# mLSTM rows stored chunk by chunk, the first head's masks spread, the first modulation in halves, and a head's queries and keys as transfers to all 128 partitions

## The chip, the core and the metric

The kernel runs as one program on one core of a Trainium2 chip. The core has five engines with instruction streams of their own: TensorE (PE in the profile; PEld is its loading of weights), VectorE (DVE), ScalarE (ACT), GpSimd (POOL) and SyncE (SP). It also has 16 DMA engines, which move data between HBM and the on-chip memory SBUF. In this kernel SP does almost nothing but issue DMAs, one behind the other, in the order of the program; GpSimd issues a few more. The metric is the device time of one execution in microseconds (us). SBUF has 128 partitions, and a tile is written here as partitions x elements.

## The reference, cut to what matters

One layer works on 2048 latent rows of 1024 features (a grid 64 wide), with 256 rows of context in front. Its steps are these:

1. A conditioning vector `c` (for the context `c_ctx`) goes through SiLU and a matrix `w_ada` to give shift, scale and gate (the modulation).
2. The normalised rows, shifted and scaled, go through one input projection `w_in`. Its columns feed two groups of heads.
3. Group A is neighbourhood attention: 8 heads of 64 features. Every latent row reads a clamped window of 8 x 16 rows with a learned bias, and all context rows, in one softmax.
4. Group B is an mLSTM: 4 heads of 128 features, in both directions, in chunks of 128 rows, with a state carried from chunk to chunk.
5. Both outputs go through an output projection, a normalisation, and a mixture of experts with another normalisation.

```
q, k, v = heads(z)                       # group A, 8 heads of 64
p = softmax([q . k_window + bias, q . k_ctx]);  o = p . [v_window, v_ctx]
for chunk in 16 chunks of 128 rows:      # group B, 4 heads of 128, two directions
    h = (decay * (q k^T)) v + q C        # C: the state so far
    C = f * C + k^T v
```

## The kernel before, in words

The stages follow each other on the core. The first modulation and the first rows take the first 41 us. The input projection runs to 793 us. The mLSTM runs from 793 to 973 us in 32 steps (16 chunks, two directions in turn). The neighbourhood attention runs from 973 to 1280 us in 8 heads of 16 blocks. The output projection and the router follow until about 1600 us, and the mixture of experts takes the rest.

The projection keeps float32 accuracy by splitting each value in a high and a low part. It leaves the attention's queries in DRAM as `qhi` and `qlo` and the keys as `khi` and `klo` (128 rows each: two heads of 64 features). The mLSTM's queries and keys lie in `mqk_d` (L57) as [128 features, 2, 4 heads, 2304 rows].

*The mLSTM loop* is at L857 to L875. Turn n fetches the operands of step n+3 (`fetch_step`, L100 to L108: `qk` from `mqk_d`, the broadcast gate rows `bcs`, the values `va`), then takes one piece of the generator `head(0)`, which loads the first attention head, and then computes. The tiles `qk` and `bcs` have three buffers each. VectorE forms the decayed weights (L796: `ex` from `bcs`, four instructions a step), multiplies them with the scores (L816) and updates the state (L784). GpSimd scales values and queries (L802, L808).

*A head's load* is the generator `head(h)` (L703 to L748). It puts, in this order, on SP's stream: `qhi` and `qlo` (64 rows of 8192 bytes each, to partitions 0-63 and 64-127 of the tile `qkk`), `khi` twice and `klo` twice (64 rows of 9216 bytes each, to both halves), nine `bias` tiles, `vc`, and sixteen pieces of the values `vw`. After the fourth bias load GpSimd adds the window's mask to a bias tile (L721), one in each further piece. The attention loop (L1047 to L1083) takes two pieces of the next head's generator in each of its turns, so a head's loads are put on SP's stream while the head before it is computed. The tiles of a head exist twice (`kps[h % 2]`).

*The order on SP* is the program's. All these loads go through one queue, and a later issue stands behind an earlier one that waits.

*Transfers with a written-out source.* Some loads name their source as a list of [step, count] pairs, outermost first. A bias load (L732) has 16 x 8 rows of 384 or 512 elements. The gates are read back for the mLSTM's scans (L273, L274) as 4 heads x 16 chunks x 128 elements, to 64 partitions:

```
src = bass.AP(tensor=gd.tensor, offset=off, ap=[[NT, 4], [P if d == 0 else -P, n], [1, P]])
```

*The first modulation* (L185 to L220) loads `c` and `c_ctx` with one feature to a partition, then all 32 pieces of `w_ada` (128x512, 256 KB each); four products run beside each other on PE for each of eight k. Only then come four transposes, and after them the first rows are transposed and projected (L246 to L248). The weights `w_in` of the projection come by `load_w` (L227).

Of the kernel before, what the change touches and what calls it, by code (L numbers as in the profile page):

```python
# [11 lines left out]
F32 = mybir.dt.float32  # L12
# [4 lines left out]
AF = mybir.ActivationFunctionType  # L17
OP = mybir.AluOpType
# [4 lines left out]
P = 128  # L23
D = 1024
KC = D // P
SEQ = 2048
# [9 lines left out]
def tile_layer(ctx, tc, A, out):  # L36
    nc = tc.nc

    def in_order(i):
        return tc.keep_in_program_order(i)  # L40
# [11 lines left out]
    qhi_d = [dram.tile([P, SEQ], F32, name=f"qhi{i}") for i in range(4)]  # L52
    qlo_d = [dram.tile([P, SEQ], F32, name=f"qlo{i}") for i in range(4)]
# [3 lines left out]
    mqk_d = dram.tile([P, 2, 4, NT], F32, name="mqk_d")  # L57
# [54 lines left out]
    with ExitStack() as es, ExitStack() as zes:  # L112
# [72 lines left out]
        def first_modulation():  # L185

            cc = stp.tile([P, 2, KC], F32, name="cc", bufs=1)
            nc.sync.dma_start(cc[:, 0, :], A["c"].rearrange("o (k p) -> p (o k)", p=P))
            nc.sync.dma_start(cc[:, 1, :], A["c_ctx"].rearrange("(k p) -> p k", p=P))
            nc.gpsimd.memset(cs[:], 0.0)  # L190
            for i in range(2):
                nc.scalar.activation(cs[:, :, i], cc[:, i, :], AF.Silu)
            pa = pt.tile([P, 2, 2, P], F32, name="ptx")
            pa = pa[:].rearrange("p a b t -> p (a b t)")
            for i in range(2):
                bada = zp.tile([1, 1024], F32, name=("cosq", "sinq")[i])
                nc.sync.dma_start(bada[:], A["b_ada"][:, i * 1024 : (i + 1) * 1024])
                for j in range(2):
                    c0 = 64 * i + 32 * j
                    nc.tensor.matmul(  # L200
                        pa[c0 : c0 + 32, :], ones1[:], bada[:, j * 512 : (j + 1) * 512], start=True, stop=False, tile_position=(0, c0)
                    )
            for k in range(KC):
                wts = []
                for j in range(4):
                    wt = xg.tile([P, 512], F32, name=f"x{('hi', 'lo')[j // 2]}_{j % 2}_{k}")
                    nc.sync.dma_start(wt[:], A["w_ada"][0, k * P : (k + 1) * P, j * 512 : (j + 1) * 512])
                    wts.append(wt)
                for j in range(4):
                    nc.tensor.matmul(  # L210
                        pa[32 * j : 32 * j + 32, :], cs[:, k, :], wts[j][:], start=False, stop=k == KC - 1, tile_position=(0, 32 * j)
                    )
            rows = tp.tile([P, 512], F32, name="t")
            nc.vector.tensor_copy(rows[:], pa)
            pm = pt.tile([P, 2, 2, P], F32, name="ptx")
            pm = pm[:].rearrange("p a b t -> p (a b) t")
            for q in range(4):
                nc.tensor.transpose(pm[:, q, :], rows[:, q * P : (q + 1) * P], ident[:])
            nc.vector.tensor_copy(modT[:, :, 0:64], pm[:, :, 0:64])
            nc.vector.tensor_scalar(modT[:, :, 64:P], pm[:, :, 64:], 1.0, None, OP.add)  # L220

        def weights(c0):

            his, los = [], []
            return his, los, c0
# [146 lines left out]
        def context_state():  # L372
# [3 lines left out]
            for i in range(2):  # L376
                c = 16 + i
                nc.sync.dma_start(kt[:, i], mqk_d[:, 1, :, c * P : (c + 1) * P])
                nc.gpsimd.memset(va[i][:, :, 128:129], 1.0)
                nc.sync.dma_start(va[i][:, :, 0:P], mv_d[c * P : (c + 1) * P, :].rearrange("p (h d) -> p h d", h=4))  # L380
# [98 lines left out]
        def rows_of_x(half, q):  # L479
            r0 = half * 1024 + q * 512  # L480
            return load_rows(A["x"][0, r0 : r0 + 512], 4, (["x"] * 3 + spare)[4 * q :])

        xq = [normalised(rows_of_x(0, 0))]
        first_modulation()
# [10 lines left out]
        for half in range(2):  # L495
# [18 lines left out]
            w = weights(0)  # L514
            if half:
                load_w(w)
            for q, (g, n, t0) in enumerate(groups[0:2]):
                pss = []
                for k2 in range(0, KC + 2, 2):
                    if half == 0 and q == 0 and k2 < KC:  # L520
                        load_w(w, (k2, k2 + 1))
                    built(g, k2 // 2 + 1)
                    if half or k2 == KC:
                        built(groups[1][0], k2 // 2 + 1 if half else 1)
                    if k2 == 2:
                        pss = [pz.tile([P, 512], F32, name="ps") for _ in range(4)]
                    if k2:
                        for c in range(4):
                            mm_T(pss[c][:], g, w, c * P, (k2 - 2, k2 - 1))
                    if half == 0 and q == 0 and k2 == 2:  # L530
                        rows_of[1] = normalised(rows_of_x(0, 1), True)
# [58 lines left out]
            for qk in range(2):  # L590
# [5 lines left out]
                for h in range(4):  # L596
# [3 lines left out]
                    for g, n, t0 in groups:  # L600
# [38 lines left out]
                        if t0 == SEQ:  # L639
                            nc.vector.tensor_scalar(acc[:, 0:m], acc[:, 0:m], P ** -0.5, None, OP.mult)  # L640
                            nc.sync.dma_start(mqk_d[:, 1, h, SEQ:NT], acc[:, 0:m])
                            continue
# [7 lines left out]
                        nc.sync.dma_start(mqk_d[:, qk, h, o0:o1], t1[:, 0:m])  # L650
# [47 lines left out]
    heads = {}  # L698

    def load(dst, src):  # L700
        in_order(nc.sync.dma_start(dst, src))

    def head(h):  # L703
# [5 lines left out]
        load(q[0:64, :].bitcast(F32), qhi_d[pair][f0 : f0 + 64, :])  # L709
        yield  # L710
        load(q[64:P, :].bitcast(F32), qlo_d[pair][f0 : f0 + 64, :])
        yield
        for dst, src in ((ka, khi_d), (kb, klo_d)):
            for p0 in (0, 64):
                load(dst[p0 : p0 + 64, :].bitcast(F32), src[pair][f0 : f0 + 64, :])
            yield
        bias = []

        def masked(i):
            w = (12, 16, 12)[i // 3] * 32  # L720
            in_order(nc.gpsimd.tensor_tensor(bias[i][:, 0:w], bias[i][:, 0:w], mask[:, i, 0:w], OP.add))  # L721
# [186 lines left out]
    with ExitStack() as es:  # L908
# [139 lines left out]
        for n in range(128 + 6):  # L1048
# [1171 lines left out]
```

## Time and profile before

| | |
|---|---|
| time, median of 3 runs | 2725.88 us (2724.01 to 2726.02) |
| the profiled execution's own time | 2719.89 us |
| its span, first to last instruction | 2717.9 us |
| mean granted clock of TensorE | 0.962 |
| PE, DVE, ACT, POOL busy | 91%, 47%, 30%, 28% of the span |
| DMA traffic, mean | 231 GB/s |

PE is busy for most of the span as a whole, but the stages differ. The share of the span says nothing of a single stage; each is read by itself, from its own stretch, with the wait that ends last there. The chain of waits that ended last, in the page, holds only the last DMAs of the mixture of experts, so it tells nothing of the stages in which the change lies.

### The profile page before, as it was taken

Reading aid. Unit: us, or ns where it says so; the run is one execution under the profiler, and the core shown is the slowest. Engines: PE = TensorE matmul, PEld = TensorE weight load, DVE = VectorE, ACT = ScalarE, POOL = GpSimd, SP = SyncE. Lnnn points to the kernel's source line nnn. Section 1 sums busy time; section 2 is a strip of 40 time slices with the busy share of each in tenths; the row PEclk is TensorE's granted clock in tenths of the full one; section 3 lists DMA queues with packets and bytes.
Section 4 is the critical chain, followed back from the end, with each engine's and each line's share of the span. In section 5 each row is a group of like instructions: output and inputs, shape, how many; then the busy total and the mean of one; then the engine's idle time right before and its main releaser. Section 6 shows DMA issues by size and latency. Waiting matters only on the chain. (4 is left out here: it accounts for less than half of the span.)

```text
span 2717.9 us, 51820 instructions
## 1 busy us (share of the span) xinstructions
PE 2481.7 (91%) x17292; PEld 1568.7 (58%) x17292; DVE 1268.3 (47%) x2882; ACT 804.9 (30%) x1707; POOL 759.1 (28%) x886
## 2 busy tenths in 40 slices
PE   8999999999997899998999679979999999999890
PEld 4778667877887778876787533323333333333330
DVE  5547224257236976665578952222222233222226
ACT  4423105243134666655565310000000000000005
POOL 1212211002034535456434422211222122221124
PEclk9999999999999999999999779989999999999995
DMA  8634762334449979994654689999689886998936
GB/s 268 178 102 134 248 219 94 140 97 158 112 137 260 265 197 214 202 212 141 183 152 151 213 308 349 366 394 340 220 281 335 312 299 223 331 328 318 381 102 263
DMA packets 286891, 626.97 MB, mean 231 GB/s; under 512 B 79448, under 2 KB 142924, under 8 KB 262444
## 3 DMA queue, kind: packets, MB, share of 16 engines
q1 hardware_dynamic: 254716, 564.87, 62.6%
q0 software_dynamic: 31696, 60.09, 9.6%
q8 instruction: 70, 1.15, 0.2%
q10 hardware_dynamic: 352, 0.39, 0.1%
q14 instruction: 57, 0.47, 0.1%
HBM read 947.01 MB, written 97.42 MB: 384 GB/s over the span
## 5 line engine op out<-in xcount | busy, mean ns | idle before, releaser
L2048 POOL DMA_INDIRECT acc_d<-y,ids x112 | 174.6, 1559 | 739.9 <-DMA acc_d<-y,ids 277.7
L2011 DVE TENSOR_TENSOR sg<-sg,ph 128x128 f32<-128x128 f32 x112 | 39.8, 355 | 442.7 <-ACT sg L2010 427.2
L2010 ACT ACTIVATE sg<-ph 128x128 f32<-128x128 f32 x112 | 37.1, 331 | 690.5 <-PE ph L2005 522.3
L2005 PE MATMUL ph<-qkk,xT 128*64 128x512 f32 (+1 forms) x1344 | 233.9, 525 | 2.8 <-DMA qkk<-in_w_dram 2.8
L2005 PE MATMUL ph<-mask,xT 128*64 128x512 f32 x896 | 210.8, 613 | 21.5 <-DMA mask<-in_w_dram 21.5
L246 PE MATMUL ps<-xhi,whi 128*128 128x512 f32 (+1 forms) x576 | 221.7, 386 | 1.7 <-DVE ev L509 1.6
L247 PE MATMUL ps<-xlo,whi 128*128 128x512 f32 (+1 forms) x576 | 220.4, 383 | 0.2 <-DVE xlo L182 0.2
L248 PE MATMUL ps<-xhi,wlo 128*128 128x512 f32 (+1 forms) x576 | 220.2, 382 | 0.0
L2037 PE MATMUL py<-mo,gT 128*64 128x512 f32 x672 | 166.2, 631 | 24.4 <-DMA mask<-in_w_dram 12.3
L255 PE MATMUL ps<-whi,xhi 128*128 128x512 f32 x416 | 166.1, 401 | 1.5 <-ACT whi L234 1.5
L256 PE MATMUL ps<-wlo,xhi 128*128 128x512 f32 x416 | 164.3, 396 | 3.2 <-DVE wlo L235 3.2
L257 PE MATMUL ps<-whi,xlo 128*128 128x512 f32 x416 | 164.8, 397 | 0.0
L960 DVE CUSTOM_DVE_ANT_0 sb<-ps,bias 128x640 f32<-128x640 f32 (+1 forms) x128 | 113.9, 891 | 102.9 <-PE ps L957 82.7
L2005 PEld LDWEIGHTS ph<-mask,xT 128*64 128x64 f32 x896 | 61.8, 140 | 144.5 <-issue 142.8
L2005 PEld LDWEIGHTS ph<-qkk,xT 128*64 128x64 f32 (+1 forms) x1344 | 74.9, 128 | 114.4 <-issue 98.5
L2021 DVE COPY gT<-pg 128x128 f32<-128x128 f32 x112 | 40.2, 359 | 210.6 <-PE pg L2019 205.7
L1972 DVE TENSOR_SCALAR xT<-pxt,mod 128x96 f32<-128x96 f32 x456 | 135.0, 369 | 2.5 <-PE pxt L1965 2.5
L246 PEld LDWEIGHTS ps<-xhi,whi 128*128 128x128 f32 x576 | 108.3, 188 | 28.7 <-issue 3.2
L2045 DVE SCALAR_TENSOR_TENSOR y<-py,wgt,g2r 128x256 f32<-128x256 f32 x112 | 68.7, 613 | 119.9 <-PE py L2037 119.9
L2010 ACT ACT_TABLE_LOAD x28 | 35.9, 1283 | 299.5 <-PE ph L2005 299.5
L247 PEld LDWEIGHTS ps<-xlo,whi 128*128 128x128 f32 x576 | 108.3, 188 | 23.0 <-DVE xlo L182 0.9
L248 PEld LDWEIGHTS ps<-xhi,wlo 128*128 128x128 f32 x576 | 108.3, 188 | 23.0 <-DVE wlo L235 0.3
(549 smaller groups left out, 5087.2 us busy)
## 6 DMA issues: line engine op xcount, KB each, us to landing
w<-in_w_dram SPq DMA_DIRECT2D x203, 1024.0 KB, 7.5
mask<-in_w_dram SPq DMA_DIRECT2D x114, 1024.0 KB, 8.7
qkk<-in_w_dram SPq DMA_DIRECT2D x114, 1024.0 KB
mo<-in_w_dram SPq DMA_DIRECT2D x171, 512.0 KB, 4.1
bias<-in_w_dram SPq DMA_DIRECT2D x58, 1024.0 KB
xo<-in_w_dram SPq DMA_DIRECT2D x115, 512.0 KB, 8.2
bias<-in_w_dram SPq DMA_DIRECT2D x58, 512.0 KB
qkk<-in_w_dram SPq DMA_DIRECT2D x58, 512.0 KB
```

What stands on the lines that cost most here:

```text
L246: nc.tensor.matmul(ps, wh_, xhi[g, k][:], start=k == 0, stop=False)
L247: nc.tensor.matmul(ps, wh_, xlo[g, k][:], start=False, stop=False)
L248: nc.tensor.matmul(ps, wl_, xhi[g, k][:], start=False, stop=k == KC - 1)
L255: nc.tensor.matmul(ps, xh, his[k], start=k == 0, stop=False)
L256: nc.tensor.matmul(ps, xh, los[k], start=False, stop=False)
L257: nc.tensor.matmul(ps, xl, his[k], start=False, stop=k == KC - 1)
L960: in_order(nc.vector.tensor_tensor_reduce(out=sb[:, 0:L], in0=ps[:, off:768], in1=bt[:, 0:L], scale=-0.125, scalar=3.0e38, op0=OP.add, op1 ...
L1972: i = nc.vector.tensor_scalar(xT[u][:, k], pxt[:, k, 0:96], mod2[:, 1, k : k + 1], mod2[:, 0, k : k + 1], OP.mult, OP.add)
L2005: in_order(nc.tensor.matmul(ph[j * n : (j + 1) * n], xT[u][:, k, t0 : t0 + n], w13[k][:, :, j * NH : (j + 1) * NH], start=k == 0, stop=k = ...
L2010: nc.scalar.activation(sg[:], ph[:, 0, :], AF.Silu)
L2037: in_order(nc.tensor.matmul(py[j * n : (j + 1) * n, :], gT[:, b_, j_ * n : (j_ + 1) * n], w2t[c][:, j * NY : (j + 1) * NY], start=c == 0, ...
L2048: sc = nc.gpsimd.indirect_dma_start(out=acc_d[:].rearrange("t (g n) -> (t g) n", g=G), out_offset=bass.IndirectOffsetOnAxis(ap=ids[u][:, l ...
```

## The change

It has four parts.

1. `mqk_d` becomes [18 chunks, 128, 2, 4, 128]. The fetch of a step reads 128 rows of 4096 bytes in place of 1024 pieces of 512 bytes. The stores of the rows (the new `mqk_store`) write pieces of 512 bytes, in two DMAs where a stretch does not end on a chunk.
2. The first modulation is made in two halves: `c` and `c_ctx` come as 16 rows of 128 features and are transposed on PE; sixteen pieces of `w_ada` and three of `w_in` come first, the other sixteen after them in between further pieces of `w_in`; the rows are transposed and the first products run between the halves.
3. Of the first head's nine masks, three are added on VectorE in the mLSTM loop, and six on GpSimd in the first turns of the attention loop.
4. A head's queries come as one DMA whose source has the shape [2, 64, 2048] and whose destination is 128 partitions; `khi` and `klo` come as one DMA each, source [2, 64, 2304] with a step of 0 on the first axis. Three loads of a head stand in place of six.

```diff
@@ the tables in DRAM
-    qhi_d = [dram.tile([P, SEQ], F32, name=f"qhi{i}") for i in range(4)]
-    qlo_d = [dram.tile([P, SEQ], F32, name=f"qlo{i}") for i in range(4)]
+    q_d = [dram.tile([2, P, SEQ], F32, name=f"q{i}") for i in range(4)]
+    qhi_d, qlo_d = ([t[i] for t in q_d] for i in range(2))
-    mqk_d = dram.tile([P, 2, 4, NT], F32, name="mqk_d")
+    mqk_d = dram.tile([NT // P, P, 2, 4, P], F32, name="mqk_d")
+    def mqk_store(qk, h, o0, o1, src):
+        while o0 < o1:
+            c, a = o0 // P, o0 % P
+            n = (o1 - o0) // P if a == 0 else 0
+            if n:
+                nc.sync.dma_start(
+                    mqk_d[c : c + n, :, qk, h, :].rearrange("c p t -> p c t"), src[:, 0 : n * P].rearrange("p (c t) -> p c t", t=P)
+                )
+                m = n * P
+            else:
+                m = min(P - a, o1 - o0)
+                nc.sync.dma_start(mqk_d[c, :, qk, h, a : a + m], src[:, 0:m])
+            o0, src = o0 + m, src[:, m:]
@@ fetch_step
-        in_order(nc.sync.dma_start(qk[:], mqk_d[:, :, :, c * P : (c + 1) * P]))
+        in_order(nc.sync.dma_start(qk[:], mqk_d[c]))
@@ first_modulation
-            for k in range(KC):
...
-                    wt = xg.tile([P, 512], F32, name=f"x{('hi', 'lo')[j // 2]}_{j % 2}_{k}")
-                    nc.sync.dma_start(wt[:], A["w_ada"][0, k * P : (k + 1) * P, j * 512 : (j + 1) * 512])
...
+            nc.scalar.activation(cc[:], cc[:], AF.Silu)
...
+            nc.tensor.transpose(pc, cc[:], ident[0 : 2 * KC, 0 : 2 * KC])
...
+            for part in range(2):
...
+                        nc.sync.dma_start(wt[:], A["w_ada"][0, k * P : (k + 1) * P, c0 : c0 + 512])
...
+                if part == 0:
+                    yield
@@ head
-        load(q[0:64, :].bitcast(F32), qhi_d[pair][f0 : f0 + 64, :])
+        def rows_twice(t, step, n):
+            return bass.AP(tensor=t.tensor, offset=t.offset + f0 * n, ap=[[step, 2], [n, 64], [1, n]])
+        load(q.bitcast(F32), rows_twice(q_d[pair][:], P * SEQ, SEQ))
         yield
-        load(q[64:P, :].bitcast(F32), qlo_d[pair][f0 : f0 + 64, :])
         yield
         for dst, src in ((ka, khi_d), (kb, klo_d)):
-            for p0 in (0, 64):
-                load(dst[p0 : p0 + 64, :].bitcast(F32), src[pair][f0 : f0 + 64, :])
+            load(dst.bitcast(F32), rows_twice(src[pair][:], 0, NT))
             yield
...
-            in_order(nc.gpsimd.tensor_tensor(bias[i][:, 0:w], bias[i][:, 0:w], mask[:, i, 0:w], OP.add))
+            e = nc.vector if h == 0 and i < 3 else nc.gpsimd
+            add = lambda: in_order(e.tensor_tensor(bias[i][:, 0:w], bias[i][:, 0:w], mask[:, i, 0:w], OP.add))
+            if h == 0 and i >= 3:
+                first_masks.append(add)
+            else:
+                add()
@@ the attention loop
+            if n < len(first_masks):
+                first_masks[n]()
```

The first place is SP's stream in the mLSTM loop, where the first head's loads stand between the fetches of the steps (`qk`, `bcs` and `va` are one fetch; `qkk` is the head's tile). Before:

```order
L701 DMA qkk<-qlo_72 64x2048
L104 DMA qk<-mqk_d 128x8x128
L106 DMA bcs<-bc_d 128x512
L108 DMA va_5959<-mv_d 128x4x128
L701 DMA qkk<-khi_76 64x2304 x2
L104 DMA qk<-mqk_d 128x8x128
L106 DMA bcs<-bc_d 128x512
L108 DMA va_5960<-mv_d 128x4x128
L701 DMA qkk<-klo_80 64x2304 x2
```

And now:

```order
L750 DMA qkk<-q_68 128x1x2048
L120 DMA qk<-mqk_d 128x1024
L122 DMA bcs<-bc_d 128x512
L124 DMA va_5982<-mv_d 128x4x128
L120 DMA qk<-mqk_d 128x1024
L122 DMA bcs<-bc_d 128x512
L124 DMA va_5983<-mv_d 128x4x128
L750 DMA qkk<-khi_72 128x1x2304
L120 DMA qk<-mqk_d 128x1024
L122 DMA bcs<-bc_d 128x512
L124 DMA va_5984<-mv_d 128x4x128
L750 DMA qkk<-klo_76 128x1x2304
```

A fetch still stands between any two of the head's loads, and behind the queries now come two fetches; the pairs of 64 rows have become single loads of 128.

The second place is SP's stream at the start of a later head in the attention loop. Before:

```order
L701 DMA qkk<-qhi_69 64x2048
L701 DMA qkk<-qlo_73 64x2048
L701 DMA qkk<-khi_77 64x2304 x2
L701 DMA qkk<-klo_81 64x2304 x2
L701 DMA bias<-rel_d 128x1x384 x3
L701 DMA bias<-rel_d 128x1x512 x3
L701 DMA bias<-rel_d 128x1x384 x3
L701 DMA vc<-nv_d 128x2x64
L701 DMA vw_8838<-nv_d 32x8x64 x4
```

And now:

```order
L750 DMA qkk<-q_69 128x1x2048
L750 DMA qkk<-khi_73 128x1x2304
L750 DMA qkk<-klo_77 128x1x2304
L750 DMA bias<-rel_d 128x1x384 x3
L750 DMA bias<-rel_d 128x1x512 x3
L750 DMA bias<-rel_d 128x1x384 x3
L750 DMA vc<-nv_d 128x2x64
L750 DMA vw_8853<-nv_d 32x8x64 x4
```

Three loads stand where six stood, and the bias, `vc` and `vw` follow them as they did.

The third place is VectorE's stream in the mLSTM loop, one step with what surrounds it (`C` is the state, `ex` the weights, `ps` the scores). Before:

```order
L784 SCALAR_TENSOR_TENSOR C_6734<-C_6610,dec,pu 128x129 x4
L816 TENSOR_TENSOR ex<-ex,ps 128x512
L796 SCALAR_TENSOR_TENSOR ex<-bcs,cols,cmask 128x128 x4
L836 SCALAR_TENSOR_TENSOR rc<-pn,cols 128x4
L837 TENSOR_TENSOR rc<-rc,pn 128x4
L838 RECIPROCAL rc<-rc 128x4
```

And in one of the three steps that now hold a mask:

```order
L840 SCALAR_TENSOR_TENSOR C_6755<-C_6631,dec,pu 128x129 x4
L773 TENSOR_TENSOR bias<-bias,mask 128x384
L872 TENSOR_TENSOR ex<-ex,ps 128x512
L852 SCALAR_TENSOR_TENSOR ex<-bcs,cols,cmask 128x128 x4
L892 SCALAR_TENSOR_TENSOR rc<-pn,cols 128x4
L893 TENSOR_TENSOR rc<-rc,pn 128x4
L894 RECIPROCAL rc<-rc 128x4
```

The addition of the mask to a bias tile stands between the state's update and the product of weights and scores; the same addition is gone from GpSimd's stream there.

## Rows read from the trace of the kernel before

**Rows 1.** Stages; from:to, length, each engine's busy us (count), PEclk, DMA share, GB/s.
```profile
300.00:640.00 340.00, 338.10 (x1501) 247.29 (x1501) 138.05 (x217) 104.60 (x165) 43.48 (x69) 1.00 0.47 155
820.00:857.00 37.00, 25.38 (x174) 24.47 (x173) 15.76 (x60) 15.49 (x47) 12.45 (x14) 0.86 1.03 250
909.00:970.00 61.00, 54.51 (x432) 49.92 (x432) 60.17 (x160) 40.86 (x126) 28.77 (x25) 1.00 0.81 240
1008.00:1145.00 137.00, 136.86 (x1276) 112.71 (x1276) 93.71 (x194) 84.66 (x203) 67.19 (x95) 1.00 0.95 214
```

**Rows 2.** Tile sb on VectorE: count, duration min/median/max in ns, first and last start.
```profile
L960 DVE CUSTOM_DVE_ANT_0 sb<-ps,bias x128: 806/889/959, 974.9 to 1273.6; 128x640 f32<-128x640 f32 x64, 128x768 f32<-128x768 f32 x64
```

**Rows 3.** Waits of VectorE, 795 to 975 us: total us, times, longest us.
```profile
DVE ex L796 <- DMA bcs<-bc_d: 21.7, 5, 7.5
```

**Rows 4.** Line L815 on PE in the mLSTM loop, two stretches (steps 6 and 10).
```profile
L815 PE MATMUL ps<-qk x6: 274/275/275, 819.9 to 820.5; 128*128 128x128 f32 x6
...
L815 PE MATMUL ps<-qk x3: 275/275/347, 853.3 to 853.6; 128*128 128x128 f32 x3
```

**Rows 5.** DMA view, 574.6 to 576.7 us: 40 slices, busy tenths of 16 engines.
```profile
DMA  0122211222322210041111122211133222320000
GB/s 10 59 88 68 59 49 49 78 68 88 98 78 78 78 29 0 20 29 39 39 59 39 59 68 59 59 39 39 59 98 98 78 78 88 98 68 20 20 0 0
q1 hardware_dynamic: 244, 0.12, 19.6%
xlo<-gates_d SPq DMA_DIRECT2D x2, 32.0 KB
```

**Rows 6.** DMA view, 12 to 36 us.
```profile
DMA  8978989999999999999999999999999999999999
GB/s 287 304 236 273 266 215 256 352 399 410 406 403 399 389 393 393 389 386 382 393 386 382 386 382 382 389 382 403 386 386 389 393 382 382 382 386 382 393 382 434
```

**Rows 7.** DMA view, 1043 to 1059 us.
```profile
DMA packets 613, 3.56 MB, mean 222 GB/s; under 512 B 132, under 2 KB 229, under 8 KB 229
q1 hardware_dynamic: 580, 3.54, 99.6%
```

**Rows 8.** Timeline of SP's queue: start, length in us, line, transfer.
```profile
807.89 0.74 SPq L701 DMA_DIRECT2D qkk<-qhi  x1
...
818.55 2.05 SPq L701 DMA_DIRECT2D qkk<-khi  x2
...
828.92 1.76 SPq L701 DMA_DIRECT2D qkk<-klo  x2
...
975.45 0.48 SPq L701 DMA_DIRECT2D qkk<-qhi  x1
...
1045.61 16.67 SPq L701 DMA_DIRECT2D bias<-rel_d  x9
...
1062.95 11.34 SPq L701 DMA_DIRECT2D vw<-nv_d  x16
1077.16 0.47 SPq L701 DMA_DIRECT2D qkk<-qhi  x1
```

**Rows 9.** Timeline of VectorE: the state's update in four steps of the mLSTM.
```profile
861.46 1.09 DVE L784 SCALAR_TENSOR_TENSOR C<-C,dec,pu 128x129 f32<-128x129 f32 x4
862.47 0.68 DVE L816 TENSOR_TENSOR ex<-ex,ps 128x512 f32<-128x512 f32 x1
...
867.17 1.09 DVE L784 SCALAR_TENSOR_TENSOR C<-C,dec,pu 128x129 f32<-128x129 f32 x4
...
908.09 1.09 DVE L784 SCALAR_TENSOR_TENSOR C<-C,dec,pu 128x129 f32<-128x129 f32 x4
...
913.06 1.09 DVE L784 SCALAR_TENSOR_TENSOR C<-C,dec,pu 128x129 f32<-128x129 f32 x4
```

**Rows 10.** Timeline of PE: last modulation product, first and last projection product, later products.
```profile
33.85 1.73 PE L210 MATMUL ptx<-xlo,cs 128*32 128x512 f32 x4
...
40.96 1.17 PE L246 MATMUL ps<-xhi,whi 128*128 128x512 f32 x4
...
65.75 0.39 PE L248 MATMUL ps<-xhi,wlo 128*128 128x512 f32 x1
...
307.66 0.62 PE L468 MATMUL ptx<-z,cs 128*32 128x512 f32 x2
...
308.11 0.60 PE L468 MATMUL ptx<-z,cs 128*32 128x512 f32 x2
```

**Rows 11.** Tile mqk_d: who waited for it (us, times).
```profile
DVE t L647: 5.7, 6
```

More of the change, by code (lines that the diff above doesn't have):

```diff
@@ L185, in first_modulation @@
         def first_modulation():
-            cc = stp.tile([P, 2, KC], F32, name="cc", bufs=1)
-            nc.sync.dma_start(cc[:, 0, :], A["c"].rearrange("o (k p) -> p (o k)", p=P))
-            nc.sync.dma_start(cc[:, 1, :], A["c_ctx"].rearrange("(k p) -> p k", p=P))
             nc.gpsimd.memset(cs[:], 0.0)
+            cc = stp.tile([2 * KC, P], F32, name="cc", bufs=1)
+            nc.sync.dma_start(cc[0:KC, :], A["c"].rearrange("o (k p) -> (o k) p", p=P))
+            nc.sync.dma_start(cc[KC : 2 * KC, :], A["c_ctx"].rearrange("(k p) -> k p", p=P))
@@ L191, in first_modulation @@
+            bada = []
             for i in range(2):
[L192 to L202, printed above, removed]
@@ L213, in first_modulation @@
[L213 to L220, printed above, removed]
+                bada.append(zp.tile([1, 1024], F32, name=("cosq", "sinq")[i]))
@@ L377, in context_state @@
                 c = 16 + i
-                nc.sync.dma_start(kt[:, i], mqk_d[:, 1, :, c * P : (c + 1) * P])
+                nc.sync.dma_start(kt[:, i], mqk_d[c, :, 1])
                 nc.gpsimd.memset(va[i][:, :, 128:129], 1.0)
@@ L481, in rows_of_x @@
             return load_rows(A["x"][0, r0 : r0 + 512], 4, (["x"] * 3 + spare)[4 * q :])
+        first_mod = first_modulation()
+        next(first_mod)
         xq = [normalised(rows_of_x(0, 0))]
-        first_modulation()
+        next(first_mod)
+        w_first = load_w(weights(0), (0, 1))
+        next(first_mod)
         rows_of, builds = {0: xq[0]}, {}
@@ L511, in evacuated, with products @@
                 nc.sync.dma_start((qlo_d, klo_d)[qk][c][:, t0 : t0 + W], lo[:, 0:W].bitcast(F32))
-            w = weights(0)
-            if half:
-                load_w(w)
+            w = load_w(weights(0)) if half else w_first
             for q, (g, n, t0) in enumerate(groups[0:2]):
                 pss = []
[L519 to L531, printed above, removed]
+                def products(k2):
+                    for c in range(4):
+                        mm_T(pss[c][:], g, w, c * P, (k2, k2 + 1))
+                if half == 0 and q == 0:
+                    built(g, 1)
+                    load_w(w, (2, 3))
+                    built(g, 2)
+                    pss.extend(pz.tile([P, 512], F32, name="ps") for _ in range(4))
+                    products(0)
+                    load_w(w, (4, 5))
+                    products(2)
+                    load_w(w, (6, 7))
+                    next(first_mod)
+                    coming = rows_of_x(0, 1)
+                    built(g, 3)
+                    built(g, 4)
+                    products(4)
+                    rows_of[1] = normalised(coming, True)
+                    built(groups[1][0], 1)
+                    products(6)
+                else:
+                    for k2 in range(0, KC + 2, 2):
+                        built(g, k2 // 2 + 1)
+                        if half or k2 == KC:
+                            built(groups[1][0], k2 // 2 + 1 if half else 1)
+                        if k2 == 2:
+                            pss.extend(pz.tile([P, 512], F32, name="ps") for _ in range(4))
+                        if k2:
+                            products(k2 - 2)
                 for c in range(4):
@@ L640, in tile_layer @@
                             nc.vector.tensor_scalar(acc[:, 0:m], acc[:, 0:m], P ** -0.5, None, OP.mult)
-                            nc.sync.dma_start(mqk_d[:, 1, h, SEQ:NT], acc[:, 0:m])
+                            mqk_store(1, h, SEQ, NT, acc[:, 0:m])
                             continue
@@ L649, in tile_layer @@
                         nc.vector.tensor_tensor(t1[:, 0:m], t1[:, 0:m], sw[:, 0:m], OP.add)
-                        nc.sync.dma_start(mqk_d[:, qk, h, o0:o1], t1[:, 0:m])
+                        mqk_store(qk, h, o0, o1, t1[:, 0:m])
             mg = tp.tile([P, 512], F32, name="t")
```

38 lines of the change are left out of this document (32 added, 6 removed).

## The prediction, made before the changed kernel ran

> **What bounds the kernel now.** I read the table of stages first, because the change lies in four stages with different limits. The projection keeps PE busy for 338.10 of 340 us [rows 1]: there only what delays or advances its beginning counts. The steady mLSTM keeps VectorE busy for 60.17 of 61 us, while from 820 to 857 us VectorE works 15.76 of 37 us with the DMA engines full (share 1.03) [rows 1]. The waits name the cause: VectorE waits 21.7 us for `bcs`, in five waits [rows 3]. That is where the first head's load runs between the fetches. The attention keeps PE busy for 136.86 of 137 us, with the DMA engines at 0.95 [rows 1]. Its blocks take (1273.6 - 974.9)/127 = 2.35 us each, so a head of 16 takes 37.6 us [rows 2], and the next head's 3.41 MB and its bias come in just under that. So each of a head's loads has little room: a load of a head that takes longer than some 35 us becomes the bound of the attention.
>
> **The heads' loads: what the new form does.** The question is how many of the 16 DMA engines one new load uses. Its source is a nest of 2 x 64 x 2048 elements (the keys' 2 x 64 x 2304, the 2 with a step of 0). One transfer of before has a small count in front: `xlo<-gates_d` (L274) reads 4 x 16 x 128 elements into 64 rows. It never moved more than 98 GB/s, with two or three tenths of the 16 engines busy, although two of these transfers were out at once [rows 5]. With all 16 engines the pieces of `w_ada` (128 rows) move 382 to 410 GB/s [rows 6], 24 to 25.6 GB/s for each engine; 98 is four times that. So a transfer spreads over as many engines as the outermost count of its nest, here four, and two such transfers share the same four. The 64-row loads and the bias loads (nests of 16 x 8 rows) do fill the engines (99.6%), at 222 GB/s [rows 7], so neither 64 rows nor a nest of three levels holds engines idle. The nest now begins with 2, so I take two engines, 2 x 25.6 = 51.2 GB/s, the same two for all.
>
> [...]
>
> The queries are 128 x 2048 x 4 = 1.049 MB, so 20.5 us; each key load 128 x 2304 x 4 = 1.180 MB, 23.0 us. A head takes 20.5 + 23.0 + 23.0 = 66.5 us, one behind the other. Whatever SP issues after one of them has its own share on these two engines and lands behind it.
>
> **In the attention** [rows 8]. The head's other 26 loads come after the keys. SP does stall behind landings: nine bias issues took 16.67 us behind the keys of before, sixteen of `vw` 11.34 (0.71 each). I take it that some seven issues get past the last key load while it runs and 19 wait for it: 19 x 0.71 = 13.5, with 2 us for the landing and 2 for the next head's start 17.5. A head's bias (1.97 MB) and values (1.11 MB) leave a sixteenth on each engine, 0.19 MB or 7.5 us at 25.6 GB/s; half of that falls in the 17.5, and I add 3.5 for the rest. A head's period is then 66.5 + 17.5 + 3.5 = 87.5 us, and PE, which needs 37.6 of it, waits for the keys. If SP is not held at all, it is 66.5 + 3.5 = 70; if the two engines run at the 78 GB/s in which many slices of the `gates_d` transfers stood (19.5 each [rows 5]), 3.41 MB take 87, and the period is 108.
> The second head's load begins where it did, at 975.45, and ends 2 + 66.5 + 3.5 later, at 1047.5. Before, its blocks began at 974.9 + 37.6 = 1012.5: 35 late. The six heads after it come at 87.5 in place of 37.6: 6 x 49.9 = 299. The last head then runs without waiting for anything but its own blocks, -3. Sum +331, with bounds 35 + 6 x 32.4 - 3 = +226 and (35 + 21) + 6 x 70.4 - 3 = +475.
>
> **In the mLSTM.** The queries are issued at 807.89 [rows 8] and land at about 830. The fetch of step 6 stands behind them, so step 6 starts at 830, not at 819.9 [rows 4]. The first keys, issued at 818.55, then run until 855, the fetch of step 8 behind them; the second, issued at about 829, until 880, the fetch of step 9 behind them. Step 9 starts at 883, and step 10, behind the mask's load and the first bias, at 889. Before it started at 853.3 [rows 4]: +36. The masks leave GpSimd: with one, a step is 867.17 - 861.46 = 5.71 us, without 913.06 - 908.09 = 4.97 [rows 9], so nine masks give back 6.7. Three additions on VectorE cost about 0.5 each (the nearest row is 0.68 for 128x512 [rows 9], these are 128x384), 1.5. The six additions at the start of the attention, about 1 us each, lie in its first turns on GpSimd; the first head's blocks begin with tiles whose masks come first, and I cost them at 0 (up to 3). Sum +31, bounds +20 to +45. The smaller number of pieces in the fetch (1024 of 512 bytes become 128 of 4096) shortens a transfer, but where VectorE is full [rows 1] it gives nothing, and in the stall it isn't what ends last: 0, bounds -2 to 0.
>
> **At the start** [rows 6, 10]. `w_ada` takes 8.4 MB at some 390 GB/s = 21.5 us; the first half is there 10.7 us earlier. From the last product at 33.85 + 1.73 = 35.58 to the first of the projection at 40.96 lie 5.4 us of copies and transposes. The first projection product moves from 41 to about 29 (three pieces of `w_in` come before it). Its 48 product groups take 25 us to 66. In between come 18 products of the second half, at the pace of the later ones (four in 0.45 us) 2 us, at one by one up to 18 x 0.45 = 8, and a second chain of 5.4, partly beside PE's work. So the end of this group comes at 61 to 68 in place of 66. The loads of `c` in 4-byte pieces also go. I take -3, bounds -8 to +4; PE is full behind it, so it passes on.
>
> **The stores of `mqk_d`** become 16 times as many pieces in the projection, where PE is bound [rows 1] and DMA is half idle; VectorE waited 5.7 us for these stores [rows 11]. +1, bounds 0 to +3.
>
> **Sum.** 331 + 31 - 3 + 1 = +360. The profiled execution took 2719.89 us, its span 2717.9; 2719.9 + 360 = 3080, and the median of the runs stands 6 us above the profiled one: 3086, say 3085.
>
> **The rivals.**
> *All 16 engines at full rate: faster.* The place is the head's load; what decides is whether a nest that begins with 2 reaches all 16 engines. If it does, loads to 128 partitions run at 390 in place of 222 GB/s [rows 6, 7]: 3.41 MB take 8.7 instead of 15.4 us. The four steps from 819.9 to 853.3 [rows 4] take 33.4 us where four of 4.97 take 19.9, so between 6.7 and 13.5 are won there, say 10; masks 5; start 3; attention, where PE is full, about 2. That is -20: 2706 on the median. For it speaks the rate of the 64-row loads; against it the `gates_d` rows.
> [...]
> *Two engines, but not always the same two.* The three loads of a head then run side by side, in 23 us; with 17.5 behind them and their start a period is about 45, 6 x 7.4 = +44 in the attention, and about +20 in the mLSTM: 2790. Against it: two `gates_d` transfers together did not pass 98 GB/s [rows 5].
> *Nothing from the new loads:* they take what the six took. Then only masks and start count, -8 or less, and with a slower start about none: 2718 to 2726.
>
> **How the numbers follow.** Two engines, the same two: 0.85. All 16: 0.08. Changing pairs: 0.05. Nothing: 0.02, half of it faster. A measurement of this kernel can tell about 0.2% (5.4 us) from no change. So faster 0.09, same 0.01, slower 0.90. The first case alone: the sum of the low bounds is 226 + 20 - 2 - 8 = +236, which is 2962 on the median, of the high ones 475 + 45 + 4 + 3 = +527, 3253. Not all ends come together, so I set the upper end where the two engines run at 22.5 GB/s each: 76 us for a head's loads, a period of 97, seven times 9.5 more than the likeliest, 3152, and some margin: 3170. The range 2960 to 3170 leaves out the other cases (15 in 100) and a few of this one.
>
> **What would show it.** Right: while `qkk` loads run, the DMA view shows about 50 GB/s at one or two tenths, and a load lands 20 to 25 us after it starts; VectorE waits some 55 us for `bcs` or PE for `qk` in the mLSTM; a head's period in the attention is 80 to 95 us with PE busy for some 40% and waiting for a DMA into `qkk`; the mLSTM steps that held a mask on GpSimd take 4.97 us; the first projection product is at 27 to 31 us. Wrong: a DMA view that is full during the head's loads, or two key loads landing together, or blocks still 2.35 us apart.

## The result, and the profile after

The changed kernel takes 3083.43 us (median of 4 runs, 3081.47 to 3087.07), the kernel before 2725.86 in the same runs: a ratio of 1.1315, 95% interval 1.1295 to 1.1335. The forecast was 3085, range 2960 to 3170. Its profiled execution took 3084.47 us, its span is 3082.6. From the traces the 364.7 us by which the span grew divide like this:

| stretch | before | after | difference | forecast |
|---|---|---|---|---|
| to the first product of the mLSTM | 793.4 | 783.5 | -9.8 | -3 + 1 |
| from there to its step 10 | 59.9 | 105.4 | +45.4 | +36 |
| from step 10 to the attention's first block | 121.6 | 114.6 | -7.0 | -5 |
| first to last block of the attention | 298.7 | 627.0 | +328.3 | +331 |
| from there to the end | 1444.3 | 1452.1 | +7.8 | 0 |

The table of stages after, with the columns of [rows 1] and the same stretches of time, shows the limits gone in the second and the fourth of them; the other two are as full as before:

```profile
300.00:640.00 340.00, 337.75 (x1505) 248.05 (x1506) 140.09 (x218) 106.48 (x167) 45.26 (x70) 1.00 0.47 153
820.00:857.00 37.00, 11.65 (x80) 11.52 (x81) 8.48 (x30) 6.66 (x21) 5.43 (x6) 0.64 0.29 99
909.00:970.00 61.00, 54.11 (x442) 50.47 (x442) 60.17 (x154) 39.47 (x120) 29.42 (x27) 1.00 1.02 288
1008.00:1145.00 137.00, 66.80 (x590) 54.42 (x588) 44.09 (x90) 40.00 (x95) 18.78 (x27) 0.75 0.24 81
```

From 820 to 857 us and from 1008 to 1145 us nothing is full: PE, VectorE and the DMA engines are all far from busy (DMA shares 0.29 and 0.24). Such a stretch waits for something with a rate of its own. The DMA view of 1006 to 1046 us, just behind the issue of the second head's first loads, shows it (40 slices of 1 us; compare [rows 5 to 7]):

```profile
DMA  0111211111111111111111111111111111111111
GB/s 25 49 57 49 66 57 57 49 57 57 49 49 57 57 49 49 57 74 49 49 55 55 54 46 55 55 55 55 55 46 46 55 55 55 55 55 55 55 46 55
q1 hardware_dynamic: 243, 2.09, 12.4%
```

A flat tenth: SP's queue has 12.4% of the 16 engines' time, which is 1.98 engines, and moves 2.09 MB in 40 us. That is 52 GB/s, 26 for each of two engines. (243 packets for 2.09 MB are 8.6 KB each; most slices of 1 us hold five to seven of them, so they alternate around that mean.) The queries and the first keys had both been issued by 1005.13 us and were out together, so no second pair of engines took a part of them. SP's queue after (answers to [rows 8]):

```profile
1003.97 0.56 SPq L750 DMA_DIRECT2D qkk<-q  x1
1004.59 0.54 SPq L750 DMA_DIRECT2D qkk<-khi  x1
1005.18 18.30 SPq L750 DMA_DIRECT2D qkk<-klo  x1
1023.58 51.84 SPq L750 DMA_DIRECT2D bias<-rel_d  x9
1075.52 0.54 SPq L750 DMA_DIRECT2D vc<-nv_d  x1
1076.10 8.45 SPq L750 DMA_DIRECT2D vw<-nv_d  x16
1084.65 0.52 SPq L750 DMA_DIRECT2D qkk<-q  x1
...
1170.61 0.53 SPq L750 DMA_DIRECT2D qkk<-q  x1
...
1253.74 0.53 SPq L750 DMA_DIRECT2D qkk<-q  x1
```

SP is held: the low keys' own issue takes 18.30 us, and the nine bias issues behind it take 51.84 where they took 16.67 [rows 8]. The bias issues end at 1075.42 us, 1.1 us after PE goes on with the low keys (1074.29). From head to head it is 80.7, 86.0 and 83.1 us. The blocks of the attention (answers to [rows 2]) and the two largest waits of PE there (from 1000 to 1650 us, columns as in [rows 3]):

```profile
L1016 DVE CUSTOM_DVE_ANT_0 sb<-ps,bias x128: 808/888/959, 1003.5 to 1630.5; 128x640 f32<-128x640 f32 x64, 128x768 f32<-128x768 f32 x64
```

```profile
PE ps L1009 <- DMA qkk<-klo: 167.3, 7, 24.3
PE ps L1009 <- DMA qkk<-khi: 138.5, 6, 26.4
```

PE waits seven times for the low part of a head's keys and six times for the high part, 306 us in all. VectorE's blocks wait 335 us for the masked bias, which is not a second cause: the bias loads stand behind the keys on SP, and in the second head the first masked bias is ready at 1075.81 us, 0.4 us after the scores. In the mLSTM the waits of [rows 3] after, first VectorE's, then PE's, are:

```profile
DVE ex L852 <- DMA bcs<-bc_d: 68.4, 4, 24.4
```

```profile
PE ps L871 <- DMA qk<-mqk_d: 57.5, 3, 21.2
```

And the steps themselves, PE's timeline after (steps 0, 6, 8, 9, 10; answers to [rows 4]; the bracket is the idle time before and its cause), with step 0 of the kernel before in a fence of its own:

```profile
783.53 0.72 PE L871 MATMUL ps<-qk 128*128 128x128 f32 x5
...
825.74 0.55 PE L871 MATMUL ps<-qk 128*128 128x128 f32 x1 [16.68 <-DMA qk<-mqk_d]
...
855.17 1.20 PE L871 MATMUL ps<-qk 128*128 128x128 f32 x4 [19.61 <-DMA qk<-mqk_d]
...
882.80 0.98 PE L871 MATMUL ps<-qk 128*128 128x128 f32 x3 [21.20 <-DMA qk<-mqk_d]
...
888.92 0.84 PE L871 MATMUL ps<-qk 128*128 128x128 f32 x6
```

```profile
793.36 0.49 PE L815 MATMUL ps<-qk 128*128 128x128 f32 x3
```

Three fetches, each 17 to 21 us late: one behind the queries, one behind each key load. SP is held in this stage, too, in the issues of the fetches and of the low keys:

```profile
797.24 0.57 SPq L750 DMA_DIRECT2D qkk<-q  x1
...
804.15 10.24 SPq L120 DMA_DIRECT2D qk<-mqk_d  x1
...
832.61 12.15 SPq L750 DMA_DIRECT2D qkk<-klo  x1
844.87 8.19 SPq L120 DMA_DIRECT2D qk<-mqk_d  x1
```

### The profile page after: what moved, and what is told of

It is laid out like the page before. It is cut to its first block, busy times and chain, and to the rows that moved or that the text cites. A ratio compares the mean times of both kernels' runs of the same rounds, so it can differ in the third digit from the quotient of the medians.

```text
span 3082.6 us, 51803 instructions
## 1 busy us (share of the span) xinstructions
PE 2495.9 (81%) x17297; PEld 1583.1 (51%) x17297; DVE 1257.9 (41%) x2889; ACT 805.4 (26%) x1706; POOL 760.0 (25%) x883
## 5 line engine op out<-in xcount | busy, mean ns | idle before, releaser
L1009 PE MATMUL ps<-qkk 128*128 128x384 f32 (+1 forms) x256 | 96.5, 455 | 321.1 <-DMA qkk<-klo 167.3
L1009 PEld LDWEIGHTS ps<-qkk 128*128 128x128 f32 x256 | 42.6, 205 | 344.5 <-DMA qkk<-klo 170.1
L773 POOL TENSOR_TENSOR bias<-bias,mask 128x384 f32<-128x384 f32 (+1 forms) x69 | 75.8, 1117 | 355.3 <-DMA bias<-rel_d 355.3
L1038 ACT COPY pT<-pb 128x128 f32<-128x128 f32 (+1 forms) x128 | 40.7, 318 | 425.5 <-PE pb L1035 425.4
```

Source lines behind the costliest of these rows:

```text
L1009: in_order(nc.tensor.matmul(ps[:, off:512], ql, kg[i][:, R0[rb] : R0[rb] + nr, C0[cb] : C0[cb] + 32], start=i == 0, stop=i == 1))
```

## The experiments

Medians are compared with runs of the kernel before on the same chips (2724 to 2727 us). Where intervals are given, they are of the ratio.

**1. Six loads again, the other parts kept** (five rounds).

```diff
-        load(q.bitcast(F32), rows_twice(q_d[pair][:], P * SEQ, SEQ))
+        load(q[0:64, :].bitcast(F32), qhi_d[pair][f0 : f0 + 64, :])
         yield
+        load(q[64:P, :].bitcast(F32), qlo_d[pair][f0 : f0 + 64, :])
         yield
         for dst, src in ((ka, khi_d), (kb, klo_d)):
-            load(dst.bitcast(F32), rows_twice(src[pair][:], 0, NT))
+            for p0 in (0, 64):
+                load(dst[p0 : p0 + 64, :].bitcast(F32), src[pair][f0 : f0 + 64, :])
```

> The changed kernel with a head's six loads of 64 rows put back; the other three parts stay. Theory (two engines carry the new loads, and that is the whole loss): the blocks of the attention are 2.35 us apart again; what is left of the change is the earlier start of the projection (5.6 us) and the steps of the mLSTM that hold no mask on GpSimd any more (11 us from step 10 on): 2709 us, 2700 to 2718. Rival (a good part of the loss comes from the other parts: the stores of 512-byte pieces, the masks at the start of the attention, the order at the start): above 2800 us.

Measured: 2702.21 us, ratio 0.9914 [0.9893, 0.9936]. The blocks are back at their old distance (2.32 us, before 2.35), and the other three parts gain 23 us by themselves, inside the expected range but more than its middle; the blocks:

```profile
L1014 DVE CUSTOM_DVE_ANT_0 sb<-ps,bias x128: 807/888/959, 958.6 to 1253.8; 128x640 f32<-128x640 f32 x64, 128x768 f32<-128x768 f32 x64
```

**2. The new loads alone, in the kernel before** (three rounds). The edit is the reverse of experiment 1, in the kernel before, with `q_d` for the queries.

> The kernel before with only the new loads of a head (source 2 x 64 x n). Theory: the attention grows by some 328 us as in the changed kernel, the mLSTM by some 45 (from step 4 to step 10 it lost 45 in the changed kernel): 3100 us, 3085 to 3115, more than the changed kernel. Rival (other parts hold much of the loss): below 2950 us.

Measured: 3100.65 us, ratio 1.1377 [1.1347, 1.1408]: the loads alone cost 375 us. The attention's blocks:

```profile
L962 DVE CUSTOM_DVE_ANT_0 sb<-ps,bias x128: 805/884/959, 1021.9 to 1650.7; 128x640 f32<-128x640 f32 x64, 128x768 f32<-128x768 f32 x64
```

628.8 us from first to last, as in the changed kernel (627.0). Experiments 1 and 2 nearly add up: 375 - 23 = 352 against 358.

**3. The nest with 64 in front** (five rounds). One line differs from the changed kernel:

```diff
-            return bass.AP(tensor=t.tensor, offset=t.offset + f0 * n, ap=[[step, 2], [n, 64], [1, n]])
+            return bass.AP(tensor=t.tensor, offset=t.offset + f0 * n, ap=[[n, 64], [step, 2], [1, n]])
```

The rows of the high and the low part now alternate over the partitions, in queries and keys alike, so the sum over partitions has the same terms.

> The changed kernel, each head's three loads with the first two levels of the source swapped (64 x 2 x n in place of 2 x 64 x n): the same bytes to the same 128 partitions, rows of the high and the low part in turn. Theory (the outermost count sets the number of engines): all 16 engines, near 390 GB/s while a head's loads run, the stall of the mLSTM at the loads goes, 2698 us, 2688 to 2708. Rival A (loads to 128 partitions, or rows read twice, are slow by themselves): 3083 as the changed kernel. Rival B (all 16 engines, but no faster than 64-row loads, 222 GB/s): as with six loads, about 2709.

Measured: 2679.89 us, ratio 0.983 [0.9807, 0.9854]: faster than both kernels, and 8 us below the expected range. The same rows are read and the same 128 partitions are written, though a row now goes to another partition; the two counts have changed places, and some 400 us go. The DMA view of 1045 to 1052 us, while a head's queries and keys come in:

```profile
DMA  9398669999797979997949696949595959394949
DMA packets 385, 2.84 MB, mean 405 GB/s; under 512 B 56, under 2 KB 64, under 8 KB 64
```

405 GB/s in place of 52 with two in front, and of some 222 with 64 rows. VectorE's waits for `bcs` in the mLSTM, and the blocks:

```profile
DVE ex L852 <- DMA bcs<-bc_d: 15.9, 15, 2.5
```

```profile
L1016 DVE CUSTOM_DVE_ANT_0 sb<-ps,bias x128: 810/887/959, 942.1 to 1224.7; 128x640 f32<-128x640 f32 x64, 128x768 f32<-128x768 f32 x64
```

No wait for `bcs` in the mLSTM is over 2.5 us, and the blocks are 2.23 us apart (282.6 in place of 298.7). Rivals A and B are both out. It is also 22 us better than six loads, so the loads to all 128 partitions are worth that once they run at 405 GB/s.

**4 and 5. Counts of four and eight in front, six loads of 64 rows** (three rounds each). From experiment 1, every source becomes a nest of the same 64 rows in another order:

```diff
+        def by_four(t, n):
+            return bass.AP(tensor=t.tensor, offset=t.offset + f0 * n, ap=[[n, 4], [4 * n, 16], [1, n]])
...
-                load(dst[p0 : p0 + 64, :].bitcast(F32), src[pair][f0 : f0 + 64, :])
+                load(dst[p0 : p0 + 64, :].bitcast(F32), by_four(src[pair][:], NT))
```

> The changed kernel with six loads of 64 rows of a head again, but each with a source nest of 4 x 16 x n (the rows in another order, the same for queries and keys). Theory (four engines, 4 x 27.5 = 110 GB/s): a head's 3.41 MB take 31 us, a head's period in the attention is 31 + 21 = 52 us in place of 83, DMA view near 110 GB/s: about 2800 us, 2770 to 2830. Rival (any nest of three levels drops to two engines, or the speed depends on the rows): 3083. Rival (64-row loads always use all engines): 2709.

> As the kernel with 4 x 16 x n, six loads of 64 rows, but with a nest of 8 x 8 x n. With a count of four the loads moved some 90 GB/s (22.5 for each engine) and a head's period was 59 us = 38 + 21. Theory (eight engines, 180 GB/s): 19 + 21 = 40 us for a head against 35.4 with all engines, 2702 + 6 x 4.6 = 2730, 2710 to 2745. Rival (the nest of three levels itself costs): above 2780. Rival (from four on the count doesn't matter): 2884.

Measured: 2884.26 us (1.0579 [1.055, 1.0608]) with four, 2796.85 us (1.0267 [1.0248, 1.0286]) with eight. How many engines work is read where only a head's loads run. SP's queue then has, first with four (979 to 985 us), then with eight (1069 to 1072 us):

```profile
q1 hardware_dynamic: 54, 0.43, 25.0%
```

```profile
q1 hardware_dynamic: 48, 0.39, 50.6%
```

A quarter of the 16 engines' time is four engines, a half is eight. SP's bias issues behind the loads, with four and with eight:

```profile
1033.78 44.22 SPq L750 DMA_DIRECT2D bias<-rel_d  x9
...
1089.16 1.14 SPq L750 DMA_DIRECT2D qkk<-q  x2
```

```profile
1019.61 34.48 SPq L750 DMA_DIRECT2D bias<-rel_d  x9
...
1067.10 1.26 SPq L750 DMA_DIRECT2D qkk<-q  x2
```

A larger count holds SP less (51.84, 44.22, 34.48, 16.67 us for two, four, eight and the 64 of before) and makes the kernel faster (3083, 2884, 2797, 2702). The rivals that only the rows matter, that any nest of three levels is as slow as this one, or that from four on the count doesn't matter, are out. But both sizes were missed: the kernel with four is 54 us above the top of its range, the one with eight 52 above its own. The second lies where the rival that the nest of three levels itself costs had put it (above 2780); but the engine shares account for the steps, and in experiment 3 a nest of three levels moves 405 GB/s. What was wrong is the rate of an engine. From the two rows above, four engines move 0.43 MB in 6 us, 72 GB/s or 18 each, and eight move 0.39 MB in 3 us, 130 GB/s or 16 each, where two engines had 26 each; the 64-row loads on all 16 engines have 222/16 = 14 each. So the count sets how many engines work, but not what each of them gives. Why the rate falls in the loads of 64 rows was not tried out.

**6. Only the first head with two in front** (three rounds): the nest of experiment 3 for the heads 1 to 7, that of the change for head 0.

```diff
-            return bass.AP(tensor=t.tensor, offset=t.offset + f0 * n, ap=[[step, 2], [n, 64], [1, n]])
+            return bass.AP(tensor=t.tensor, offset=t.offset + f0 * n, ap=[[step, 2], [n, 64], [1, n]] if h == 0 else [[n, 64], [step, 2], [1, n]])
```

> The changed kernel with 2 x 64 x n as the source nest for the first head alone, 64 x 2 x n for the other seven. Theory (the first head's loads cost what the mLSTM lost, the others' what the attention lost, and the two add): from the mLSTM's first step to the attention's first block the changed kernel took 220 us and the one with 64 in front 159, so 61 more than its 2680: 2741 us, 2733 to 2749, and blocks 2.2 us apart. Rival (the attention gets part of it back, or the mLSTM hides it): below 2725.

Measured: 2736.72 us, ratio 1.0029 [1.0014, 1.0043], 57 us over experiment 3, and the blocks 2.21 us apart:

```profile
L1016 DVE CUSTOM_DVE_ANT_0 sb<-ps,bias x128: 807/887/959, 1002.5 to 1283.2; 128x640 f32<-128x640 f32 x64, 128x768 f32<-128x768 f32 x64
```

The first block is at 1002.5, as in the changed kernel (1003.5), and what the first head costs stays in the mLSTM; the other seven cost the rest, 3083 - 2737 = 346. The time is inside the expected range.

**7 to 10. The three other parts alone, and two of them together** (five rounds each), each in the kernel before.

```diff
-        in_order(nc.sync.dma_start(qk[:], mqk_d[:, :, :, c * P : (c + 1) * P]))
+        in_order(nc.sync.dma_start(qk[:], mqk_d[c]))
...
-        first_modulation()
+        next(first_mod)
+        w_first = load_w(weights(0), (0, 1))
+        next(first_mod)
...
+            if n < len(first_masks):
+                first_masks[n]()
```

> The kernel before with only the new layout of the mLSTM's queries and keys (stores of 512-byte pieces, fetches of 4096-byte rows). Asked: who ends the projection 5.7 us earlier between 645 and 793 us, beside the 4 us won at the start. Theory (the layout: the last rows and the context's keys come sooner): mLSTM begins some 5 us earlier, and the shorter fetches take 2 to 5 us of the stall at the first head's loads: 2716 us, 2710 to 2722. Rival (it's the order of the start): the stores cost a little or nothing, 2722 to 2728 against 2724 of before.

> The kernel before with only the first modulation in halves. Theory (4 us at the start and no more): 2720 us, mLSTM 4 us earlier. Rival (the whole 10 us by which the mLSTM begins earlier come from the start): 2714 us, mLSTM's first product at 783.

> The kernel before with only the first head's masks spread. Theory (each mask on GpSimd cost its step 0.75 us, and the steps of the mLSTM lose that): attention begins 7 us earlier, 2717 us, 2713 to 2721. Rival (six masks at the beginning of the attention hold its blocks up): 2721 to 2727, blocks of the first head further apart.

> The kernel before with the first modulation in halves and the new layout of the mLSTM's queries and keys together, neither masks nor loads changed. In the kernels with all small parts the mLSTM begins 10 us earlier; alone, one part brought 3 and the other 2. Theory (they work together: the rows of the last stage and the first products): mLSTM's first product at 783 to 784, 2707 to 2713 us. Rival (they only add): 788, 2708 to 2716 by their medians. Rival (the masks, which lie behind it, move the order in the projection): 788 to 790, 2716 to 2722.

Measured: the layout 2721.24 us (0.9963 [0.9948, 0.9979]), the start 2719.40 (0.9969 [0.9953, 0.9984]), the masks 2720.72 (0.9972 [0.9955, 0.9989]), start and layout together 2710.30 (0.995 [0.9933, 0.9967]). Each part gains 0.3 to 0.4%, together 0.9% (experiment 1). The first product of the mLSTM comes at 791.39 with the layout, at 790.28 with the start alone, and with both at

```profile
784.75 0.94 PE L863 MATMUL ps<-qk 128*128 128x128 f32 x7
```

With both parts it is 8.6 us earlier than in the kernel before (793.36), alone 2 and 3. Single executions of kernels that are the same up to there stand at 793.05, 793.36 and 795.97, so the sum of 5 is uncertain by some 3 us; the kernels with both parts stand at 782.35 to 784.75 in five executions. The time with both parts (2710.30) lies in the range of the theory and in that of the rival that they only add; the first product is near the theory's 783 to 784. One place where the two work together is found in the traces. From 650 to 660 us PE of the kernel before holds 29 matmuls and is idle for 3.66 of 10 us (its row is in the next section). The same stretch with the layout alone, with the start alone and with both:

```profile
650.00:660.00 10.00, 8.69 (x40) 6.77 (x39) 7.71 (x8) 3.25 (x4) 3.59 (x1) 1.00 0.70 215
650.00:660.00 10.00, 6.99 (x26) 4.87 (x25) 8.61 (x8) 3.62 (x5) 2.71 (x1) 0.83 0.55 157
650.00:660.00 10.00, 9.95 (x48) 7.92 (x47) 7.69 (x9) 5.26 (x8) 2.49 (x1) 1.00 0.82 238
```

The layout narrows the gap, and both together close it. The layout's 2 us at the mLSTM's beginning are thus found, where 5 were expected; its time (2716 expected) is at the edge of its range. The start's time is the one expected (2720), with the mLSTM 3 us earlier for 4. With the masks alone, step 10 to the first block takes 116.5 us in place of 121.6, where the attention was expected 7 us earlier; the time is inside the range, and at its edge. The six masks at the start of the attention cost at most a microsecond: the first head's 16 blocks take 34.7 us in place of 33.7, all blocks 297.2 in place of 298.7.

## Why the prediction was right, point by point

**Two engines, the same two: right, and shown.** The step that carried it was to read the four engines of `gates_d` [rows 5] as the count in front of its nest. The share of busy engines carries that reading; the rate (98 GB/s as four times 24) does so less, since over the whole of [rows 5] an engine moved 18 GB/s (0.12 MB in 2.1 us at 19.6% of 16 engines). The profile doesn't name single engines. That two work is read from their share (12.4% of 16), that they are the same two for all loads from the 52 GB/s that the queries and the first keys had together. The counts of four and eight with 25.0% and 50.6% of the engines, and 64 rows with 99.6% [rows 7], bear the reading out for this kernel's loads.

**66.5 us a head: 65.** The two engines gave 52 GB/s and not 51.2; 3.41 MB at that rate are 65 us, by estimate.

**The attention, +331: +328.** From the second head on, the first block of a head comes 83.4 to 88.7 us before that of the next, 85.2 on average (timeline of VectorE); forecast 87.5. From the issue of the queries to PE's first use of the low keys it is 70 to 74 us, forecast 72, and from there to the next head's queries 10 to 14, forecast 15.5. The 2 us for a landing and the 2 for a head's start in these sums are estimates that no run shows by themselves; the 70 to 74 us are 5 to 9 more than the 65 at 52 GB/s. That SP is held by the keys' landing, the choice between 70 and 87.5, is right: the nine bias issues take 51.84 us. But nine issues and not seven get past the last keys, and the 17 behind take 9.0 us in place of 13.5. Head by head the sum holds as well: the second head begins 39 us later behind the first than it did (35 forecast), the six heads after it cost 293 (299), and the last head gains 3 (3). PE's own need was put a little high: a head whose keys are in time takes 35.4 us and not 37.6, which is the mean over all heads.

**The mLSTM's stall, +36: +45.4, a term too small.** The instants were nearly right (steps 6, 9, 10 forecast at 830, 883, 889, and step 8 at 858 if it follows its keys by 3 us as step 9 does; measured 825.7, 855.2, 882.8, 888.9), but on a loop that began 10 us earlier. The queries were forecast to land 22 us after their issue; step 6, whose fetch stands behind them, started 28.5 us after it (797.24 to 825.74). From step 6 to 8 and from 8 to 9 it took 29.4 and 27.6 us, forecast 28 and 25. That is 6.4 + 1.4 + 2.6 = 10.4. The term had no place for the fetches of the steps, which share the two engines, and it costed SP as held in the attention alone. The DMA view from 798 to 818 us (slices of 0.5 us) shows the fetches: until 806 us the engines carry those issued before and behind the queries, and only from there the flat tenth of two engines:

```profile
DMA  9999766989934952111111111111111111989722
GB/s 376 336 299 319 247 190 214 350 328 365 361 127 116 316 139 68 66 49 49 49 49 66 49 49 49 49 66 49 49 49 49 66 49 49 254 254 336 221 66 94
```

By estimate, the queries' 1.05 MB and two sixteenths of each of the two fetches behind them (1.05 MB each) are 1.31 MB for the two engines, 25 us at 52 GB/s, where 20.5 had stood. How the 10.4 divide between this and SP's holding is not shown. The larger pieces of the fetch, which the forecast put at 0, shorten its transfers by little: four steps' fetches and stores before (936 to 956 us) are 7693 packets and 5.44 MB and take 88.8% of the 16 engines' time, 17.8 us; after (957 to 977 us) 3916 packets and 5.45 MB take 86.0%, 17.2 us.

**The start and the stores, -3 + 1: -9.8, the other mis-sized term.** The first projection product moved as forecast (to 27 to 31 us, and the last of its group to 61 to 68):

```profile
26.83 0.74 PE L273 MATMUL ps<-xhi,whi 128*128 128x512 f32 x2 [0.18 <-DVE xhi L197]
...
62.98 0.40 PE L275 MATMUL ps<-xhi,wlo 128*128 128x512 f32 x1
```

That is 3 us of it, against 65.75 [rows 10]. The other 7 come later in the projection, which I had taken as bound by PE throughout, from [rows 1] up to 640 us; from 650 to 660 us PE of before is busy for only 6.34 of 10 us, beside a VectorE that is busy for 9.88:

```profile
650.00:660.00 10.00, 6.34 (x29) 4.64 (x28) 9.88 (x9) 3.39 (x4) 3.03 (x1) 1.00 0.42 101
```

In the kernel after PE is busy for 9.76 of these 10 us, so 3.4 of the 7 us are here; layout and start together close this gap (experiments 7 to 10). The last 3 to 4 us are not located, and single executions differ by as much. I had costed the layout at a loss of 1; alone it is a gain of 0.4%.

**The masks, -5: -7.0, the same sign and nearly the size.** A step that no longer holds a mask on GpSimd takes 910.92 - 905.91 = 5.01 us in the timeline of VectorE after, where [rows 9] had 5.71 and 4.97:

```profile
905.91 1.09 DVE L840 SCALAR_TENSOR_TENSOR C<-C,dec,pu 128x129 f32<-128x129 f32 x4
...
910.92 1.10 DVE L840 SCALAR_TENSOR_TENSOR C<-C,dec,pu 128x129 f32<-128x129 f32 x4
```

The 1.5 us for the three masks on VectorE did not appear: a step that holds one takes 4.96 us (895.93 to 900.89). The forecast of PE busy for some 40% of a head's period was low; it is 48% of the attention (300.54 of 627 us), at a lower clock (0.73 where it was 0.97).

**The total** came within 2 us (the span of one execution within 5), and that is luck in part: errors cancel. The mLSTM's stall is 9 too small in the forecast and the end of the kernel, at 0, 8 too small; the start and the stores are 8 too little gain, the masks 2, the attention 3. The +7.8 at the end has no known cause in the change: from the last block to the end, where the programs are the same, the profiled executions of all these kernels take 1444.3 to 1457.6 us. What the argument can claim is the mechanism and the attention's term, nine tenths of the sum.

**The rival on the other side** (all 16 engines) named what the loads would be worth: -20 in all. Experiment 3 gained 44. Its direction and its reason were right: loads to 128 partitions run at 405 GB/s against 222, 1.8 times as fast. The rival's size was half: the start brought 10 and not 3, the mLSTM 23 and not 15 (from its first product to the attention's first block 158.8 in place of 181.5), and the attention 16 and not 2. [rows 1] showed PE full until 1145 us; further on, in the attention of before, it is not, and 9 of the 16 us are in the last head, which takes 37.3 us in place of 46.3:

```profile
1230.00:1250.00 20.00, 11.02 (x81) 8.69 (x79) 6.68 (x16) 7.22 (x18) 14.33 (x18) 0.75 0.21 60
```

## What to carry to other kernels

Before a load is merged with another, look at the outermost count of its source and not only at the rows and bytes: here two in front of 64 rows took the load to an eighth of the engines (12.4% of their time), and the same two counts in the other order gave all of them (99.9%, SP's queue from 1045 to 1052 us in experiment 3). A DMA view that stands flat at a low tenth while a queue is waiting is the sign of it. Cost the issues behind a slow load as held, in every stage in which the load stands: here 52 to 55 us of SP's time for the bias of one head in the attention, and up to 12 for one load in the mLSTM.

## What the runs showed of the hardware that was not expected

The mean granted clock of PE is 1.00 from 1008 to 1145 us in the kernel before [rows 1] and 0.75 after, where PE is busy for half of that time and waits some 20 to 26 us at a stretch. Read by 4 us, the clock after is 1.00 from 1012 to 1040 us, where PE works until 1036, and 0.50 from 1044 to 1076, where it waits almost throughout. PE's busy time in the attention grew with it, for the same instructions (a few records are missing): 284.69 us from 974 to 1274 before, 300.54 from 1003 to 1630 after:

```profile
974.00:1274.00 300.00, 284.69 (x2581) 233.96 (x2581) 196.82 (x399) 178.60 (x425) 158.90 (x218) 0.97 0.85 196
```

```profile
1003.00:1630.00 627.00, 300.54 (x2569) 245.52 (x2569) 195.51 (x398) 177.14 (x421) 158.35 (x217) 0.73 0.29 92
```

As the loads set the period of a head, this should cost nothing here; no run tried it.

The rate of one DMA engine is not the same in all loads: 26 GB/s with two engines to 128 partitions (the new loads, 52 in all), 25 with 16 to 128 (experiment 3, 405 in all), and in the loads to 64 partitions 18 with four engines and 16 with eight (experiments 4 and 5, 72 and 130 in all) and 14 with 16 (the kernel before, 222 [rows 7]).
